# Low parts of weights on GpSimd from the pair loop to the end of the recurrence

## The chip, the cores and the metric

The kernel runs on one core of a Trainium2 chip, as one launch. The time is the device time of that launch in microseconds (us); less is better. TensorE (PE) does the matrix products; VectorE (DVE), ScalarE (ACT) and GpSimd (POOL) do the elementwise work; SyncE (SP) and ScalarE issue the transfers between the memory of the chip and SBUF. Each engine works off its own list of instructions in order, and waits in place when the next one is not ready.

## The reference

Two residual layers, each followed by a SwiGLU feed-forward block, over 1024 tokens of width 1024, all in float32. The first layer mixes by spatial gating and pooling and is not touched by the change. The second is RWKV-7 time mixing, and the change works there and in the feed-forward blocks that run beside it:

```python
def rwkv7_time_mix(h, ...):
    xx = shift(h) - h
    xr, xw, xk, xv, xa, xg = [h + xx * mu[i] for i in range(6)]
    r = xr @ w_r;  k = xk @ w_k;  v = xv @ w_v
    wlog = -softplus(-(w0 + tanh(xw @ w1) @ w2)) - 0.5
    a = sigmoid(a0 + (xa @ a1) @ a2)
    g = sigmoid(xg @ g1) @ g2
    kk = heads(k * k_k) / norm;  k = k * (1 + (a - 1) * k_a)
    # state: per head 64 x 64, one step per token
    #   sa = state @ (-kk);  state = state * w + sa (kk a)^T + v k^T;  y = state @ r
    y = wkv7_scan(r, exp(-exp(wlog)), k, v, -kk, kk * a)
    ...
    return (y * g) @ w_o

def swiglu(hn, w_gate, w_up, w_down):
    return (silu(hn @ w_gate) * (hn @ w_up)) @ w_down
```

## The kernel before

**Products in two parts.** TensorE runs in the fp32r format, which keeps fewer bits than float32. So each operand of a product is split into a high part (the fp32r rounding) and a low part (what the rounding left), and a product is three matmuls: high by high, high by low, low by high (`mm3`, lines 402 to 405). `split` (line 156) makes the two parts of a weight tile of 128x1024: ScalarE copies the loaded tile `raw` into the high part `whi` (line 157), and VectorE subtracts it from `raw` and writes the low part `wlo` (line 158). The tiles `raw`, `whi` and `wlo` have three buffers each. Weights are used in a fixed order, the list `plan`; `take` hands out the parts of one weight, and splits the next one and loads the one after it. Activations that were stored to memory and come back (`n0`, `n1`, `y`) go through the same list, with the low part named `alo`; weights of the down projection that go to buffers of their own have `wdhi` and `wdlo`.

**Halves and stages.** The 1024 tokens are worked on as two halves of 512. For each half the time mixing has these stages, and the feed-forward work of the other layer or the other half fills TensorE beside them:

1. The pair loop (`project`, lines 1305 to 1372). It runs over eight pairs of heads, p = 0 to 7. For each, TensorE multiplies by a block of `w_k` and one of `w_r` and by the low-rank weights; then a chain of short operations over ScalarE, GpSimd and VectorE makes decay, `ar` and `bk`: `sg` and `av` (GpSimd, line 1070), the running sum `cum` (VectorE, line 1331), exponentials (ScalarE), `ar` (VectorE, line 1354), `kkn` times `av` (GpSimd, line 1361) and from it `bk` (VectorE, line 1365). `interact` (line 1245, one pair later) is the TensorE product of `ar` and `bk` of one pair.
2. Two inversions of triangular 32x32 blocks (`invert`, line 1416), one for pairs 0 to 3, one for pairs 4 to 7. Each is a chain of 31 steps of two small VectorE operations, `it` (line 1427) and `xi` (line 1432), each waiting on the one before. It begins when `iat` has come back from memory (it needs `interact` of its last pair), and ends with a copy (line 1434) and the write of `xi` to memory (line 1436). There is one buffer `xi`: before the second inversion GpSimd clears it (memset, line 1421), which waits until the first one's write has left it.
3. The products with `w_v` (lines 1399 to 1401), eight weight tiles.
4. The recurrence (`recur`, line 1453) over eight chunks of 64 tokens, many small matmuls one after the other (lines 1475 and 1477), with feed-forward products in between. It starts with `load(0)`: transfers from the SP queue bring `ar`, `bk` and the rest of the first chunk; on that queue they stand behind the write of the second inversion's `xi`. The first matmul of the recurrence (`gram`, line 1477) needs `bk`.

**What sets the order.** The program is written in the order of `drive` and `beside`, which mix the steps of two generators; then a scheduler of the tile framework goes through it with a model of the times of each engine, and from that fixes the list of every engine before the launch. A change of engine for some instructions so also moves others that it does not name.

The element that selects the engine for a low part is the last argument of `split`:

Of the kernel before, what the change touches and what calls it, by code (L numbers as in the profile page):

```python
# [43 lines left out]
def tile_trunk(  # L44
# [8 lines left out]
    act, dve, pool, pe, sp = nc.scalar, nc.vector, nc.gpsimd, nc.tensor, nc.sync  # L53
# [53 lines left out]


    acts, dests, splits, makes = set(), {}, {}, {}

    def push(key, parts, view=lambda t: t, dest=None):
        plan.append((key, parts, view, dest))

    def load_at(i):
        if i >= len(plan) or i in raws:
            return
        if plan[i][0][0] in acts and plan[i][0][0] not in dests:
            return
        raw = wst.tile([P, D], F32, tag="raw", name="raw")
        for dst, src in plan[i][1]:  # L120
            act.dma_start(dst(raw), src)
        raws[i] = raw
# [4 lines left out]
    def split_at(i):  # L127
        if i >= len(plan) or i in ready:
            return
        load_at(i)  # L130
        if i not in raws:
            return
        key, _, view, dest = plan[i]
        if key[0] in makes:
            ready[i] = makes[key[0]](i)
            return
        raw = raws[i]
        to = (dest or whl)()
        if to is None:
            return  # L140
        hi, lo = to
        splits.get(key[0], lambda i, *t: split(*t))(key[1], view(raw), view(hi), view(lo))
        ready[i] = hi, lo

    def take(key):
        i = pos[0]
        assert plan[i][0] == key, (plan[i][0], key)
        pos[0] += 1
        split_at(i)
        load_at(i + 1)  # L150
        if i + 1 in raws:
            load_at(i + 2)
        split_at(i + 1)
        return ready.pop(i)

    def split(src, hi, lo, eng=None):
        act.activation(hi, src, AF.Copy)  # L157
        (eng or dve).tensor_tensor(out=lo, in0=src, in1=hi.bitcast(F32), op=ALU.subtract)  # L158
# [298 lines left out]
    def act_tiles(pool_, n=HT):  # L457
        return [pool_.tile([P, KT, n], F32R, tag=t, name=t) for t in ("ahi", "alo")]
# [231 lines left out]
    for h in range(2):  # L690
        hi, lo = act_tiles((xlp, actp)[h])
# [499 lines left out]
    def project(h, hn1, kp, ring, keep, before_v):  # L1191
# [3 lines left out]
        def tmp(tag, bufs=1, shape=None, dt=F32):  # L1195
            if early.get(tag):
                return early[tag].pop(0)
            return ep.tile(shape or [P, HT], dt, tag=tag, bufs=bufs, name=tag)
# [14 lines left out]
        for m in range(KT):  # L1213
# [4 lines left out]
            t = tmp(("k", "epx", "av", "sg")[m % 4], 2)  # L1218
# [3 lines left out]
        for n in range(2):  # L1222
            take(("wa2", n, h))

        twlo, talo = keep["twlo"], kp.tile([P, HT], F32R, tag="ghi", name="talo")
        act.activation(talo[rows[1]], twlo[rows[1]].bitcast(F32), AF.Copy)
        pool.memset(talo[rows[0]].bitcast(F32), 0.0)
# [160 lines left out]
        for cb in range(2):  # L1388
# [14 lines left out]
            for j in range(4):  # L1403
                t = tmp(("sg", "k", "kkn", "epx")[j], 2)
# [48 lines left out]
    def recur(h, wp, stream):  # L1453
# [271 lines left out]
        for c in range(8):  # L1725
# [3 lines left out]
                yield from post(c // 2)  # L1729
            yield BURST / 2  # L1730
        turned.pop()()
        yield 1.0

    early_o = {}
# [205 lines left out]
    nxt = {}  # L1940
    ps_es = open_psum("psp0", PROJ)
    project(0, hn1, kp, ring, keep, early("n0", "act1", xlp_es))
    for e in (ring_es, kp_es, np_es):
        e.close()
# [10 lines left out]
    prime_b, steps_b = down_steps(1, D0B[1], lambda f: whl(), hslot, True, spill_h, (next(between[0]) for _ in range(4)))  # L1955
    prime_b()
    drive(ffn(0, 1, nxt["hn"], f, D0P[:3], nd=2), recur(0, wp, in_pieces(hb_pool, 1, h_d[1, 0])), 6.2)
    wp_es.close()
    y, y_es = open_pool(name="y0", bufs=1, side="left")
# [36 lines left out]
    for e in (f_es, y_es, hb_es, ps_es):  # L1996
        e.close()
    ps_es = open_psum("psp1", PROJ)
    project(1, hn1, kp, ring, keep, early("n1", "act2", nxt["a_es"]))
    for e in (ring_es, kp_es, np_es):  # L2000
        e.close()
# [6 lines left out]
    f, f_es = open_pool(name="ffn2", bufs=1, side="right")  # L2008
    hnA = nxt["hn"]
    drive(ffn(1, 0, hnA, f, G1A[1], early=True), recur(1, wp, in_pieces(hp, 0, h_d[0, 1])), RATIO)  # L2010
    wp_es.close()
    ps_es.close()
# [48 lines left out]
```

## Time and profile before

| | |
|---|---|
| median of 3 runs | 2411.62 us (2407.74 to 2416.54) |
| the profiled execution, whole launch | 2410.52 us |
| its span from first to last instruction | 2408.8 us |
| TensorE busy in the span | 2327.8 us (97%) |
| VectorE, ScalarE, GpSimd busy | 1467.8, 947.7, 180.4 us |
| mean granted TensorE clock | 0.987 |

The span and the launch differ by 1.7 us, which lie before the first and behind the last instruction. The profile's page gives busy times and the costliest groups of instructions; a row of the timeline gives start, duration, engine, line, operation, and in brackets how long the engine had been idle and what it waited for; a row of the windows view gives, for a stretch of the span, the busy time of each engine with the number of instructions, the granted clock, the share of the transfer engines and GB/s. Lines are those of the kernel before; the kernel after has them one to three further down.

### The profile page before, as it was taken

The numbers are of one execution on the slowest core, as the hardware profiler recorded it, in microseconds if no ns is written. First come the engines' busy times: TensorE is split into PE (matmuls) and PEld (weight loads), VectorE is DVE, ScalarE is ACT, GpSimd is POOL, SyncE is SP. The second block draws the span as 40 slices with busy tenths as digits, with TensorE's granted clock in tenths as the row PEclk, the third lists the DMA queues.
The fourth block names the chain that finished last, engine by engine and source line by source line (L and its number), as shares of the span: only waits on it lengthen the run. The fifth ranks groups of instructions, "written<-read, shape, count | busy, mean of one in ns | idle before, by whom it ended". The sixth has DMA issues, their size and how long they took to land.

```text
span 2408.8 us, 37648 instructions
## 1 busy us (share of the span) xinstructions
PE 2327.8 (97%) x15315; PEld 1904.6 (79%) x15315; DVE 1467.8 (61%) x2312; ACT 947.7 (39%) x1427; POOL 180.4 (7%) x226
## 2 busy tenths in 40 slices
PE   8999999999999999989999899999899999999998
PEld 6888888888788787767867678777788787888887
DVE  6445775665568858847778758857654446434343
ACT  6233443444224755423337555423332224322223
POOL 0200000000000022001100022101100001000001
PEclk9999999999999999999999999999999999999999
DMA  5114452334765565774545565776434323433231
GB/s 180 53 46 146 149 163 84 126 101 150 276 227 192 162 180 134 224 206 146 157 131 143 173 159 146 212 223 169 133 110 134 109 81 96 138 98 99 80 106 52
DMA packets 408333, 342.73 MB, mean 142 GB/s; under 512 B 79392, under 2 KB 352928, under 8 KB 407392
## 3 DMA queue, kind: packets, MB, share of 16 engines
q10 hardware_dynamic: 266048, 195.33, 27.2%
q1 hardware_dynamic: 142112, 145.01, 19.3%
q8 instruction: 120, 1.97, 0.3%
q14 instruction: 53, 0.43, 0.1%
HBM read 263.33 MB, written 76.94 MB: 141 GB/s over the span
## 4 chain that ended last, share of the span: by engine, by line
PE 78%; DVE 8%; DMA 6%; issue 2%; ACT 2%; POOL 2%; SPq 1%; ACTq 0%; POOLq 0%; DVEq 0%
PE mm L403 17%; PE mm L404 17%; PE mm L405 17%; PE mm L734 5%; PE mm L736 5%; PE mm L735 5%; PE sm L1475 4%; DVE wlo L158 1%; DVE h L497 1%; PE yp L1475 1%; PE aux L1399 1%; PE mm L584 1%; PE mm L585 1%; PE aux L1400 1%; PE aux L1401 1%
## 5 line engine op out<-in xcount | busy, mean ns | idle before, releaser
L403 PE MATMUL mm<-ahi,whi 128*128 128x512 f32 x1376 | 543.2, 396 | 11.0 <-ACT whi L157 6.2
L404 PE MATMUL mm<-alo,whi 128*128 128x512 f32 x1376 | 542.9, 395 | 3.1 <-DVE alo L158 3.1
L405 PE MATMUL mm<-ahi,wlo 128*128 128x512 f32 x1376 | 541.6, 394 | 1.0 <-DVE wlo L158 0.9
L157 ACT ACTIVATE whi<-raw 128x1024 fp32r<-128x1024 f32 (+2 forms) x284 | 286.2, 1014 | 509.9 <-PE mm L404 385.8
L158 DVE TENSOR_TENSOR wlo<-raw,whi 128x1024 fp32r<-128x1024 f32 (+2 forms) x284 | 337.0, 1191 | 232.0 <-ACT whi L157 208.2
L403 PEld LDWEIGHTS mm<-ahi,whi 128*128 128x128 f32 x1376 | 259.8, 189 | 70.5 <-ACT whi L157 8.2
L404 PEld LDWEIGHTS mm<-alo,whi 128*128 128x128 f32 x1376 | 259.9, 189 | 60.3 <-DVE alo L158 4.5
L405 PEld LDWEIGHTS mm<-ahi,wlo 128*128 128x128 f32 x1376 | 259.9, 189 | 59.1 <-DVE wlo L158 3.1
L497 DVE TENSOR_TENSOR h<-h,mm 128x512 f32<-128x512 f32 x276 | 186.0, 684 | 158.5 <-PE mm L405 148.4
L403 PE MATMUL mm<-hidhi,wdhi 128*128 128x512 f32 x304 | 117.6, 394 | 4.8 <-ACT hidhi L962 3.0
L405 PE MATMUL mm<-hidhi,wdlo 128*128 128x512 f32 x304 | 119.3, 393 | 0.0
L404 PE MATMUL mm<-hidlo,wdhi 128*128 128x512 f32 x304 | 119.2, 393 | 0.1
L734 PE MATMUL mm<-ahi,whi 128*128 128x512 f32 x296 | 115.6, 390 | 0.0
L735 PE MATMUL mm<-alo,whi 128*128 128x512 f32 x296 | 115.2, 389 | 0.0
L736 PE MATMUL mm<-ahi,wlo 128*128 128x512 f32 x296 | 113.6, 389 | 0.0
L157 ACT ACTIVATE wdhi<-raw 128x1024 fp32r<-128x1024 f32 x42 | 43.3, 1057 | 162.2 <-PE mm L404 124.6
L959 DVE TENSOR_TENSOR sg<-sg,mm 128x512 f32<-128x512 f32 x52 | 35.7, 686 | 115.5 <-PE mm L405 115.4
L158 DVE TENSOR_TENSOR wdlo<-raw,wdhi 128x1024 fp32r<-128x1024 f32 x42 | 53.2, 1266 | 30.5 <-ACT wdhi L157 30.3
L403 PEld LDWEIGHTS mm<-hidhi,wdhi 128*128 128x128 f32 x304 | 57.1, 188 | 18.4 <-ACT hidhi L962 3.4
L405 PEld LDWEIGHTS mm<-hidhi,wdlo 128*128 128x128 f32 x304 | 57.4, 189 | 12.2 <-issue 0.3
L404 PEld LDWEIGHTS mm<-hidlo,wdhi 128*128 128x128 f32 x304 | 57.4, 189 | 12.2 <-DVE hidlo L963 0.5
L734 PEld LDWEIGHTS mm<-ahi,whi 128*128 128x128 f32 x296 | 55.6, 188 | 11.7 <-issue 0.2
(394 smaller groups left out, 4254.1 us busy)
## 6 DMA issues: line engine op xcount, KB each, us to landing
raw<-in_ffn_w_down_dram ACTq DMA_DIRECT2D x88, 512.0 KB
raw<-in_ffn_w_gate_dram ACTq DMA_DIRECT2D x74, 512.0 KB
raw<-in_ffn_w_up_dram ACTq DMA_DIRECT2D x74, 512.0 KB
hid_d<-hid SPq DMA_DIRECT2D x36, 512.0 KB
hd<-hid_d SPq DMA_DIRECT2D x26, 512.0 KB
raw<-in_ab_w_in_dram ACTq DMA_DIRECT2D x16, 512.0 KB
raw<-in_ab_w_out_dram ACTq DMA_DIRECT2D x16, 512.0 KB
raw<-in_rwkv_w_r_dram ACTq DMA_DIRECT2D x16, 512.0 KB
```

The source lines that it names most:

```text
L157: act.activation(hi, src, AF.Copy)
L158: (eng or dve).tensor_tensor(out=lo, in0=src, in1=hi.bitcast(F32), op=ALU.subtract)
L403: pe.matmul(o, whi, xhi, start=first, stop=False)
L404: pe.matmul(o, whi, xlo, start=False, stop=False)
L405: pe.matmul(o, wlo, xhi, start=False, stop=last)
L497: dve.tensor_tensor(out=H[h][:, m, :], in0=H[h][:, m, :], in1=o, op=ALU.add)
L584: pe.matmul(ops[j], xhi[:, k, sl], whi[:, kk], start=(k == 0), stop=False)
L734: pe.matmul(o, wh[:, k, :], x[0][:, k, :], start=st, stop=False, skip_group_check=True)
L735: pe.matmul(o, wh[:, k, :], x[1][:, k, :], start=False, stop=False, skip_group_check=True)
L736: pe.matmul(o, wl[:, k, :], x[0][:, k, :], start=False, stop=k == 3, skip_group_check=True)
L959: dve.tensor_tensor(out=s, in0=s, in1=o, op=ALU.mult)
L1475: i = f(*args, **kw)
```

## The change

A cell `low_on` names the engine that makes the low part when a weight of the list is split. It starts as VectorE. When `project` has taken its low-rank weights, just ahead of the pair loop, it is set to GpSimd; when the recurrence has recorded its last step, it is set back to VectorE. This happens once for each half. Low parts that are made without the list (`mix_steps`, `split_steps`, `norm_split`, hidden activations) stay on VectorE. The choice falls on everything of the list that is split in that stretch, so the returning activations `n0` and `n1` go to GpSimd too.

```diff
     acts, dests, splits, makes = set(), {}, {}, {}
+    low_on = [dve]
...
         hi, lo = to
-        splits.get(key[0], lambda i, *t: split(*t))(key[1], view(raw), view(hi), view(lo))
+        splits.get(key[0], lambda i, *t: split(*t, low_on[0]))(key[1], view(raw), view(hi), view(lo))
         ready[i] = hi, lo
...
         for n in range(2):
             take(("wa2", n, h))
 
+        low_on[0] = pool
         twlo, talo = keep["twlo"], kp.tile([P, HT], F32R, tag="ghi", name="talo")
...
                 yield from post(c // 2)
             yield BURST / 2
         turned.pop()()
+        low_on[0] = dve
         yield 1.0
```

109 subtractions of 128x1024 change engine: 89 `wlo`, 12 `wdlo` and 8 `alo`. The lists change at more places than these.

On GpSimd, at the end of the pair loop of the first half, pair 7, the list was

```order
L1070 TENSOR_SCALAR av<-av 128x512
L1337 COPY pct<-epx 128x8
L1358 TENSOR_SCALAR ar<-kkn 128x8
L1361 TENSOR_TENSOR kkn<-kkn,av 128x512
L1421 MEMSET xi 128x2048
L1469 MEMSET S 128x512
```

and is now

```order
L1339 COPY pct<-epx 128x8
L159 TENSOR_TENSOR wlo<-raw,whi 128x1024
L159 TENSOR_TENSOR alo<-raw,ahi 128x1024
L1360 TENSOR_SCALAR ar<-kkn 128x8
L1423 MEMSET xi 128x2048
L1363 TENSOR_TENSOR kkn<-kkn,av 128x512
L159 TENSOR_TENSOR alo<-raw,ahi 128x1024
L159 TENSOR_TENSOR wlo<-raw,whi 128x1024 x3
```

Beside the subtractions that came in, the memset of `xi` moved from behind the product `kkn` of pair 7 to ahead of it. The second half's list changed in the same way.

On TensorE, at the first matmul of the recurrence in the first half (`sm` is its PSUM tile), the list was

```order
L403 MATMUL mm<-hidhi,whi 128x512
L404 MATMUL mm<-hidlo,whi 128x512
L405 MATMUL mm<-hidhi,wlo 128x512
L1477 MATMUL sm<-ar,bk 64x128
L1475 MATMUL sm<-ar,bk 64x128 x31
```

and is now

```order
L404 MATMUL mm<-ahi,whi 128x512
L405 MATMUL mm<-alo,whi 128x512
L406 MATMUL mm<-ahi,wlo 128x512
L1479 MATMUL sm<-ar,bk 64x128
L1477 MATMUL sm<-ar,bk 64x128 x31
```

The matmul stood within a group of the down projection (`hid`) and now stands within the gate and up products ahead of it (`a`). Between `interact` of pair 7 and this matmul there were 288 matmuls of 128x512 in the first half and 308 in the second; there are now 225 and 230.

On VectorE, at the end of the first inversion of the first half, the last `bk` of the pair loop stood in the middle of the inversion's steps:

```order
L1354 SCALAR_TENSOR_TENSOR ar<-kkn,epx 128x8x63
L1432 TENSOR_TENSOR xi<-xi,it 128x7x25
L158 TENSOR_TENSOR alo<-raw,ahi 128x1024
L1171 TENSOR_TENSOR xlo<-mix,xhi 128x512
L1178 SCALAR_TENSOR_TENSOR mix<-hn_5522,vec,mix 128x512
L1427 TENSOR_TENSOR it<-iat,xi 128x156
L1365 TENSOR_TENSOR bk<-kkn,em 128x8x64
```

It now stands behind the inversion's closing copy:

```order
L1434 TENSOR_TENSOR xi<-xi,it 128x31
L1436 COPY xi<-xi 128x32x32
L1172 TENSOR_TENSOR xlo<-mix,xhi 128x512
L1371 TENSOR_TENSOR ar<-mm,epx 128x8x64
...
L1356 SCALAR_TENSOR_TENSOR ar<-kkn,epx 128x8x63
...
L1367 TENSOR_TENSOR bk<-kkn,em 128x8x64
```

So eleven of the inversion's small operations and its copy moved from behind this `bk` to ahead of it (rows left out are further `xlo` and `mix`).

## The prediction

> **What bounds the kernel now.** I read the busy times by stretch: the pair loop and the recurrence of each half, which the change touches, and for comparison a dense stretch.
>
> ```profile
> 842.00:992.00 150.00, 146.22 (x910) 121.15 (x909) 108.33 (x175) 81.59 (x123) 37.38 (x46) 0.99 0.66 182
> 992.00:1240.00 248.00, 234.52 (x3313) 190.66 (x3312) 171.67 (x371) 82.18 (x139) 24.77 (x23) 0.98 0.53 151
> 1382.00:1535.00 153.00, 146.75 (x899) 121.19 (x899) 105.50 (x172) 80.86 (x122) 36.47 (x43) 0.97 0.62 167
> 1535.00:1800.00 265.00, 249.91 (x3369) 204.01 (x3368) 174.01 (x367) 88.66 (x147) 24.22 (x24) 0.99 0.56 160
> 300.00:400.00 100.00, 100.00 (x443) 82.84 (x442) 67.54 (x98) 42.59 (x66) 0.00 (x0) 1.00 0.39 127
> ```
>
> The columns after the length are PE, PEld, DVE, ACT, POOL. TensorE bounds every stretch. In the four that the change touches it idles 3.8, 13.5, 6.2 and 15.1 us, 38.6 together; more than that no faster VectorE can give back. The dense row gives the price of a 128x512 matmul: 100 us / 443 = 0.226 us. Who made TensorE wait, over the whole span:
>
> ```profile
> PE sm L1475 <- DVE gt L1522: 12.6, 5, 6.7
> PE aux L1245 <- DVE bk L1365: 6.6, 5, 2.0
> PE sm L1477 <- DMA bk<-bk_d: 5.5, 2, 3.3
> ...
> PE sm L1475 <- DVE XT L1563: 2.4, 1, 2.4
> ```
>
> VectorE causes 15.0 us of it in the recurrence (`gt`, `XT`). The third row is the first matmul of each recurrence, which waits for its load; it decides below. The engine that gets the work, GpSimd, has room: 37 of 150 us busy in the pair loop. What counts is the order that it must keep, and what its reads do to VectorE.
>
> **The price of one low part.**
>
> ```profile
> L158 DVE TENSOR_TENSOR wlo<-raw,whi 128x1024 fp32r<-128x1024 f32 x254 | 316.6, 1248 | 230.8 <-ACT whi L157 207.6 <-PE aux L1320 10.6 <-PE mm L405 5.2
> L1361 POOL TENSOR_TENSOR kkn<-kkn,av 128x512 f32<-128x512 f32 x16 | 21.7, 1359 | 4.2 <-DVE ar L1354 3.1
> L1660 POOL TENSOR_TENSOR vch<-vch,bon 128x1024 f32<-128x1024 f32 x8 | 15.3, 1915 | 108.9 <-DMA vch<-v_d 96.7 <-DMA XT<-xi_d 12.2
> L668 POOL TENSOR_TENSOR zw<-zw 128x525 f32<-128x525 f32 x6 | 6.4, 1062 | 28.2 <-DVE zw L668 10.9 <-DVE zq L675 9.0 <-DVE zp L658 8.3
> ```
>
> On VectorE it is 1.25 us (1.22 undisturbed). The trace has none on GpSimd. From below it is bounded by the same size with a small second operand (1.92), from above by two of the 128x512 products (2.7); two additions of 128x525 give 2.1. A subtraction is nearest to the addition and to the full size row, so I take 2.0. [...]
>
> **The two engines hold each other up.** The rows of both, in the pair loop:
>
> ```profile
> 892.90 1.29 POOL L1361 TENSOR_TENSOR kkn<-kkn,av 128x512 f32<-128x512 f32 x1
> 893.23 2.04 DVE L158 TENSOR_TENSOR wlo<-raw,whi 128x1024 fp32r<-128x1024 f32 x1
> ...
> 916.59 0.63 POOL L1070 TENSOR_SCALAR sg<-sg 128x512 f32<-128x512 f32 x1 [5.58 <-ACT sg L1324]
> 916.61 0.70 DVE L1432 TENSOR_TENSOR xi<-xi,it 128x87 f32<-128x87 f32 x1
> 972.86 0.25 DVE L1432 TENSOR_TENSOR xi<-xi,it 128x87 f32<-128x87 f32 x1
> 959.30 4.17 POOL L1358 TENSOR_SCALAR ar<-kkn 128x8 f32<-128x8 f32 x1 [3.20 <-ACT kkn L1353]
> ```
>
> A low part on VectorE that began during a GpSimd product took 2.04 instead of 1.22. A step of the inversion took 0.70 behind a GpSimd operation and 0.25 alone; the steps wait on one another, which leaves gaps, and GpSimd got in at once with its usual 0.63. So in an inversion a GpSimd operation stops VectorE for nearly its length. A low part there would cost the chain 2.0 less about 0.25 (the step already under way) = 1.75, against 1.15 that it takes now (1.22 less an overlap with its neighbours). The engine is relieved of the instruction and pays more for it. The last row is the other case: VectorE ran filled without gaps, and GpSimd took 4.17 for what takes 0.74. [...]
>
> **Term 1: `kkn` of pair 7 behind the memset of `xi`.**
>
> ```profile
> 905.30:976.20 70.90, 12.98 (x10) 0.98 0.57 146
> 988.30:1024.30 36.00, 9.82 (x9) 1.00 0.60 186
> 1533.90:1575.60 41.70, 14.64 (x12) 1.00 0.69 209
> ...
> 963.55 1.83 POOL L1361 TENSOR_TENSOR kkn<-kkn,av 128x512 f32<-128x512 f32 x1
> 966.15 1.97 PE L1245 MATMUL aux<-ar,bk 64*64 64x64 f32 x32 [2.01 <-DVE bk L1365]
> 975.11 1.06 DVE L1434 COPY xi<-xi 128x1024 f32<-128x1024 f32 x1
> 986.75 1.82 POOL L1421 MEMSET xi<- 128x2048 f32 x1 [21.38 <-DMA xi_d<-xi]
> ...
> 1513.45 1.15 PE L1245 MATMUL aux<-ar,bk 64*64 64x64 f32 x32 [2.01 <-DVE bk L1365]
> 1522.41 1.10 DVE L1434 COPY xi<-xi 128x1024 f32<-128x1024 f32 x1
> 1530.76 1.82 POOL L1421 MEMSET xi<- 128x2048 f32 x1 [18.08 <-DMA xi_d<-xi]
> ```
>
> The first three rows are VectorE's low parts alone, in the stretches of the first inversion of the first half and of the second inversion of each half: 10, 9 and 12. `interact` of pair 7 already waits 2.0 us for `bk`, which needs `kkn`. Now `kkn` stands behind the memset, and this behind the write of the first inversion, which freed it 10.6 us after the copy in the first half (986.75 - 976.17) and 7.2 in the second. When will the copy end? It ended at 976.2; ten low parts leave VectorE, 13.0 us, and about 5 us of pair 7's work now stands behind it: 958 if GpSimd costs VectorE nothing. If all ten hold it for 1.75, it is 975.7. I take the middle, 967, plus 7.2 for the write, 1.8 for the memset, 1.3 for `kkn`, and 0.7 to the start of `interact`: 978 against 966.15, **+12 us**. The ends are +3.5 (958 and 7.2) and +24 (975.7 and 10.6). Behind `kkn` on GpSimd wait the low parts of the last `w_v` tiles, needed later than `interact`. The second half has the same list and gets the same +12.
>
> **Term 2: the recurrence starts too early in TensorE's list.**
>
> ```profile
> 988.37 0.70 DVE L1268 TENSOR_SCALAR iat<-iat 128x32 f32<-128x32 f32 x1 [2.91 <-DMA iat<-n_d]
> 1023.23 1.08 DVE L1434 COPY xi<-xi 128x1024 f32<-128x1024 f32 x1
> 1037.40 0.29 PE L1477 MATMUL sm<-ar,bk 64*64 64x128 f32 x1 [2.16 <-DMA bk<-bk_d]
> ...
> 1533.94 0.18 DVE L1268 TENSOR_SCALAR iat<-iat 128x32 f32<-128x32 f32 x1 [3.03 <-DMA iat<-n_d]
> 1574.45 1.11 DVE L1434 COPY xi<-xi 128x1024 f32<-128x1024 f32 x1
> 1588.92 0.29 PE L1477 MATMUL sm<-ar,bk 64*64 64x128 f32 x1 [3.33 <-DMA bk<-bk_d]
> ```
>
> From `interact` of pair 7 the load's way is: 22.2 us to the start of the second inversion (966.15 to 988.37), 35.9 for it, 13.1 for the write, the load of `ar` and that of `bk`, which follow one another on SP's queue: 71.2. TensorE needs 69.1 to get there and so waits 2.2. In the new list it has 63 matmuls fewer ahead, 14.2 us: it arrives after 54.9. The inversion loses nine low parts (9 times 1.15 less rounding, 9.1 us: 26.8), and GpSimd's are made meanwhile: TensorE's work left over in that time, 54.9 - 22.2 = 32.7, uses six weight tiles of 24 matmuls (5.4 us), and two `alo` come with them; eight times 1.75 is 14.0: 40.8. The load lands after 22.2 + 40.8 + 13.1 = 76.1, a wait of 21.2, **+19.0 us**. With GpSimd for nothing it is 62.1, a wait of 7.2 and +5.0; with 2.0 a piece +21.
>
> Second half: 20.5 to the inversion, 41.6, 13.4; TensorE's 72.1 shrink by 78 matmuls (17.6) to 54.5. The inversion: 41.6 - 13.7 + 14.0 = 41.9. The wait is 75.8 - 54.5 = 21.3, less the 3.3 of now: **+18.0**, between +4.0 and +20.
>
> **Term 3: relief.** In the recurrence `gt` and most of VectorE's work reads PSUM, and about thirty low parts a half leave it. Of the 15.0 us that TensorE waits for VectorE there I take 12 as won, between 0 and 15. The longest (6.7) is one wait. The other low parts of the pair loop and the recurrence lie beside TensorE's work, made two tiles ahead; uncovered, each would cost up to 2.0.
>
> **Sum.** 12 + 19 + 12 + 18 - 12 = +49 on the profiled launch of 2410.5, which lies 1.1 below the median: **2459.5 us**. Its own range from the ends of the terms is 2411 to 2500.
>
> **Rivals.**
> 1. *The scheduler's order holds* (on the other side). It decides if GpSimd's low parts don't stop the inversions. With the low ends, 3.5 + 5 + 3.5 + 4 - 15 = +1; and if write and loads land as early as the new lists suppose, the waits at `bk` (4.0) and at the loads (5.5) go as well: -24.5. Middle 2399. For it: in the first half the transfer engines were 60% busy during the second inversion, and the lists before met the chip within 2 to 3 us. Against it: the rows 0.70 and 2.04.
> 2. *GpSimd stands in line in the recurrence.* Its low parts stand behind products `vch` that waited 97 us in all for their transfers, and behind the memsets of `XT`. If each of the eight `vch` holds the next weight up by 3.5 us beyond its lead, 28 us come on top: 2487. Against it: TensorE's place in its list frees these waits.
> 3. *GpSimd starves*, as in the 4.17 row: then the inversions are short (low ends, 16 us), but low parts come late; half of 3.4 us for eight in each half is 27: 2410.5 + 16 + 27 - 12 = 2441.
>
> **Chances.** Forecast 0.45, rival 1 0.27, rival 2 0.16, rival 3 0.12. A difference under 0.3% (7.2 us) can't be told from none. Faster holds most of rival 1, 0.19; within, 0.11; slower, 0.70. The range over the cases is 2403 to 2490: it leaves out the better half of rival 1 and the end of rival 2.
>
> **What would show it.** Right: TensorE's waits for `bk` at `interact` of pair 7 of some 14 us, released by GpSimd's `kkn` behind the memset; waits for the load of `bk` of about 20 us at the first matmul of each recurrence; steps `it` and `xi` stretched to about 2 us beside GpSimd's low parts of 1.9 to 2.3; VectorE's busy time down by about 130 us less what the stops add. Wrong: second inversions under 30 us, or a launch under 2411.

## The result, and the profile after

The change makes the kernel slower: 2490.14 us (median of 4 runs, 2484.62 to 2492.22) against 2411.76 us, a ratio of 1.0318 with a 95% interval of 1.0297 to 1.0339. The forecast was 2459.5; the time lies at the upper edge of the range, 2403 to 2490. The direction was right, and 78 us were lost where 48 were forecast.

The profiled execution of the changed kernel has a span of 2487.3 us, 78.5 more than before. Its page begins with the busy times:

```profile
PE 2348.4 (94%) x15315; PEld 1918.8 (77%) x15315; DVE 1481.2 (60%) x2203; ACT 948.0 (38%) x1427; POOL 440.2 (18%) x335
```

VectorE has 109 instructions fewer and is busy for 13.4 us *more* than before. TensorE does the same 15315 matmuls in 20.6 us more (2348.4 against 2327.8), at a granted clock of 0.972 instead of 0.987, and idles 57.9 us more.

To see where the time went I cut each half into three stretches that begin and end at the same instructions: A from the first `interact` to that of pair 7, B from there to the first matmul of the recurrence, C from there to the end of the recurrence (its last matmul, `sm` from `ysb`). The windows view of the kernel before:

```profile
861.00:966.10 105.10, 101.37 (x681) 83.60 (x681) 80.66 (x133) 55.83 (x87) 28.44 (x33) 1.00 0.58 150
966.10:1037.40 71.30, 69.09 (x329) 57.19 (x329) 52.29 (x106) 27.48 (x36) 3.51 (x6) 0.98 0.76 227
1037.40:1234.90 197.50, 186.96 (x3105) 151.88 (x3106) 131.20 (x282) 65.61 (x118) 23.93 (x20) 0.97 0.51 145
1403.00:1513.40 110.40, 105.44 (x680) 87.02 (x680) 82.72 (x136) 56.18 (x87) 28.78 (x34) 0.95 0.57 147
1513.40:1588.90 75.50, 72.14 (x348) 59.64 (x349) 55.58 (x110) 30.38 (x39) 3.05 (x5) 1.00 0.79 228
1588.90:1796.00 207.10, 195.32 (x3128) 159.12 (x3129) 129.56 (x274) 67.48 (x122) 23.00 (x20) 0.98 0.52 146
```

and of the changed kernel:

```profile
863.30:983.90 120.60, 105.56 (x672) 86.61 (x671) 92.46 (x135) 57.62 (x90) 61.22 (x49) 0.93 0.55 141
983.90:1055.50 71.60, 56.38 (x265) 46.19 (x266) 52.20 (x73) 20.39 (x25) 34.12 (x18) 0.88 0.64 188
1055.50:1268.00 212.50, 193.06 (x3121) 157.05 (x3121) 130.37 (x263) 67.73 (x122) 56.35 (x34) 0.95 0.49 141
1444.30:1568.80 124.50, 105.77 (x674) 87.26 (x673) 94.32 (x136) 57.80 (x90) 63.35 (x49) 0.92 0.54 138
1568.80:1643.60 74.80, 56.93 (x271) 46.74 (x271) 53.62 (x73) 21.83 (x26) 36.66 (x18) 0.89 0.59 170
1643.60:1859.00 215.40, 203.03 (x3134) 164.74 (x3135) 119.77 (x251) 70.57 (x126) 75.49 (x42) 0.96 0.51 146
```

The lists differ, so a stretch doesn't hold the same number of matmuls. I charge the difference at 0.226 us a matmul: stretch B of the first half lasts as long as before, but does 64 matmuls fewer, which are 14.5 us of work put off. The forecast's relief of 12 is split evenly over the two halves.

| | A | B | C | sum |
|---|---|---|---|---|
| first half, forecast | +12 | +19 | -6 | +25 |
| first half, measured | 15.5 + 2.0 = +17.5 | 0.3 + 14.5 = +14.8 | 15.0 - 3.6 = +11.4 | +43.7 |
| second half, forecast | +12 | +18 | -6 | +24 |
| second half, measured | 14.1 + 1.4 = +15.5 | -0.7 + 17.4 = +16.7 | 8.3 - 1.4 = +6.9 | +39.1 |

Together 82.8, against a loss of 78.5; the rest lies outside, above all between the two halves, where the changed kernel wins 4.0 by the same count. A and B come out at 64.5 where 61 were forecast. The 30 us that the forecast lacks lie in C, the recurrence: the relief of 12 didn't come, and 18 were lost there instead.

TensorE's waits in the changed kernel, over the whole span:

```profile
PE sm L1479 <- DMA bk<-bk_d: 31.4, 2, 17.2
PE aux L1247 <- DVE bk L1367: 27.2, 6, 7.2
PE sm L1477 <- ACT uv L1599: 8.2, 2, 8.0
PE sm L1477 <- DVE gt L1524: 8.1, 3, 4.0
...
PE sm L1477 <- DVE Q L1577: 4.9, 3, 3.1
...
PE sm L1477 <- DVE XT L1565: 4.0, 5, 1.7
PE sm L1477 <- DVE w L1551: 4.0, 1, 4.0
```

The first is the first matmul of each recurrence (5.5 before), the second is `interact` (6.6 before), the third was 1.2 before. `gt` has fallen from 12.6, but the three other waits for VectorE in the recurrence have grown: `Q` from 0.2, `XT` from 2.4, and `w` wasn't among them. The four together are 21.0 us, where they were 15.2.

**Who holds whom in A and B.** GpSimd's and VectorE's rows, in the first and then in the second inversion of the first half:

```profile
940.27 2.44 POOL L159 TENSOR_TENSOR wlo<-raw,whi 128x1024 fp32r<-128x1024 f32 x1 [1.87 <-ACT whi L158]
940.43 2.83 DVE L1367 TENSOR_TENSOR bk<-kkn,em 128x512 f32<-128x512 f32 x1
943.32 1.97 PE L1247 MATMUL aux<-ar,bk 64*64 64x64 f32 x32 [7.00 <-DVE bk L1367]
...
1020.58 2.56 POOL L159 TENSOR_TENSOR wlo<-raw,whi 128x1024 fp32r<-128x1024 f32 x1 [1.70 <-ACT whi L158]
1020.47 0.41 DVE L1434 TENSOR_TENSOR xi<-xi,it 128x240 f32<-128x240 f32 x1
1020.91 2.50 DVE L1429 TENSOR_TENSOR it<-iat,xi 128x247 f32<-128x247 f32 x1
```

A step of 0.41 becomes 2.50 beside a low part of 2.56, and `bk`, 0.68 before, becomes 2.83: what VectorE starts during these two subtractions of GpSimd ends only 0.3 and 0.6 us after they have ended. TensorE, at `interact` of pair 5, has waited 7.0 us by then. GpSimd's low parts in the two second inversions (rows of that line alone), and the ends of these inversions:

```profile
995.10:1045.10 50.00, 0.00 (x0) 27.86 (x11) 0.99 0.56 169
1573.60:1632.90 59.30, 0.00 (x0) 35.43 (x14) 0.99 0.56 165
...
995.17 0.18 DVE L1270 TENSOR_SCALAR iat<-iat 128x32 f32<-128x32 f32 x1 [0.83 <-DMA iat<-n_d]
1044.09 1.01 DVE L1436 COPY xi<-xi 128x1024 f32<-128x1024 f32 x1
```

Eleven and fourteen low parts stand in them (28 and 35 us of GpSimd), and they last 49.9 us (995.17 to 1045.10; 36.0 before) and 59.2 us (41.6 before), although VectorE makes no low part of a weight there any more. Within these lengths VectorE also idles until the rest of `iat` has come, 0.9 us in the first half and 6.6 in the second; before the change it didn't.

**Who holds whom in C.** One place in the first half's recurrence, followed over three engines:

```profile
1109.85 2.38 POOL L159 TENSOR_TENSOR wlo<-raw,whi 128x1024 fp32r<-128x1024 f32 x1
1124.22 1.90 POOL L1662 TENSOR_TENSOR vch<-vch,bon 128x1024 f32<-128x1024 f32 x1 [12.00 <-DMA vch<-v_d]
1126.08 2.34 POOL L159 TENSOR_TENSOR wlo<-raw,whi 128x1024 fp32r<-128x1024 f32 x1
...
1128.45 0.39 ACTq L122 DMA_DIRECT2D raw<-in_ffn_w_up_dram  x1
1128.94 0.59 ACT L1599 ACTIVATE uv<-sm 64x512 f32<-64x512 f32 x1 [8.72 <-POOL wlo L159]
...
1129.58 0.48 PE L1477 MATMUL sm<-uv,bkt 128*64 128x64 f32 x2 [7.95 <-ACT uv L1599]
```

GpSimd's product `vch` waits 12.0 us for its transfer. The low part behind it starts when it is done, and frees its tile `raw` at 1128.4. ScalarE issues the loads of weights, and its next load command (the ACTq row) wants that tile; behind the command stands the copy `uv`, and for `uv` TensorE waits 7.95 us. So a low part that is late on GpSimd stops TensorE through ScalarE's list, though no matmul waits for that low part. That the load command waits for this tile is read from the times: it starts 0.03 us after the low part has ended.

### The profile page after: what moved, and what is told of

Same layout as the page of the kernel before. It is cut to its first block, busy times and chain, and to the rows that moved or that the text cites. A ratio compares the mean times of both kernels' runs of the same rounds, so it can differ in the third digit from the quotient of the medians.

```text
span 2487.3 us, 37691 instructions
## 1 busy us (share of the span) xinstructions
PE 2348.4 (94%) x15315; PEld 1918.8 (77%) x15315; DVE 1481.2 (60%) x2203; ACT 948.0 (38%) x1427; POOL 440.2 (18%) x335
## 3 DMA queue, kind: packets, MB, share of 16 engines
q10 hardware_dynamic: 266048, 195.33, 26.5%
q8 instruction: 120, 1.97, 0.3%
## 4 chain that ended last, share of the span: by engine, by line
PE 72%; DVE 14%; DMA 6%; ACT 3%; issue 2%; POOL 2%; SPq 1%; ACTq 1%; POOLq 0%; DVEq 0%
PE mm L404 16%; PE mm L405 16%; PE mm L406 16%; PE mm L735 5%; PE mm L737 5%; PE mm L736 5%; PE sm L1477 4%; DVE it L1429 3%; DVE xi L1434 3%; DMA raw<-y_d 1%; DVE xlo L1172 1%; DVE mix L1179 1%; PE yp L1477 1%; POOL wlo L159 1%; ACT whi L158 1%
## 5 line engine op out<-in xcount | busy, mean ns | idle before, releaser
L159 DVE TENSOR_TENSOR wlo<-raw,whi 128x1024 fp32r<-128x1024 f32 (+2 forms) x195 | 222.5, 1146 | 166.5 <-ACT whi L158 158.0
L404 PEld LDWEIGHTS mm<-ahi,whi 128*128 128x128 f32 x1376 | 261.4, 190 | 69.4 <-ACT whi L158 5.3
L159 POOL TENSOR_TENSOR wlo<-raw,whi 128x1024 fp32r<-128x1024 f32 x89 | 218.7, 2459 | 241.5 <-ACT whi L158 230.0
L409 POOL TENSOR_TENSOR nrs<-nrs,small 128x4 f32<-128x4 f32 x8 | 8.5, 1067 | 508.2 <-DVE nrs L445 508.2
L1789 POOL TENSOR_TENSOR u<-turn,fgb 128x512 f32<-128x512 f32 x8 | 11.5, 1433 | 377.7 <-ACT fsq L1786 357.4
L1429 DVE TENSOR_TENSOR it<-iat,xi 128x31 f32<-128x31 f32 (+15 forms) x124 | 76.0, 613 | 3.5
L1434 DVE TENSOR_TENSOR xi<-xi,it 128x31 f32<-128x31 f32 (+15 forms) x124 | 72.0, 580 | 3.4
```

Source lines behind the costliest of these rows:

```text
L404: pe.matmul(o, whi, xhi, start=first, stop=False)
L1429: dve.tensor_tensor(out=t, in0=bc(iat[:, j, j + 1 : 32].unsqueeze(2), sh), in1=bc(xi[:, j, 0 : j + 1].unsqueeze(1), sh), op=ALU.mult,)
L1434: dve.tensor_tensor(out=xs, in0=xs, in1=t, op=ALU.add)
```

## The experiments

Three theories were set against one another. **Port**: while GpSimd reads the two tiles of a low part, VectorE is kept out. **Order**: the new lists are what costs, the recurrence's early place in TensorE's list above all. **Line**: in the recurrence a low part stands in GpSimd's list behind work that waits, and holds ScalarE's list. The last was formed after the first four runs. All runs are compared with the kernel before, run on the same chip (2409 to 2413 us).

### Only the pair loop, only the recurrence

```diff
 # the pair loop only (on the change), in recur
+        low_on[0] = dve
         load(0)
 # the recurrence only (on the change), in project and in recur
-        low_on[0] = pool
         twlo, talo = keep["twlo"], kp.tile([P, HT], F32R, tag="ghi", name="talo")
...
+        low_on[0] = pool
         load(0)
```

> GpSimd makes the low parts only from the pair loop to the end of w_v; the recurrence has them on VectorE again. Set against each other at equal work done by TensorE, the two traces so far lose about 20 and 18 us in the pair loops, 23 and 23 at the first recurrence matmuls, and win back 4 and 1 in the recurrences. Theory 'port' (GpSimd's low parts keep VectorE out, in the inversions above all): nearly all of the loss stays, 2411.7 + 84 less what the recurrences lose themselves, 2485 to 2497. Rival 'recurrence' (the weights that GpSimd makes beside the recurrence are what comes late): most of the loss is gone, under 2450.

> GpSimd makes the low parts only in the recurrence. In TensorE's list the first recurrence matmul stands 273 and 272 big matmuls behind the last interact, against 288 and 308 before and 225 and 230 in the change. Theory 'port': the relief of 5 us (4 and 1) stays, 2403 to 2410, and both second inversions are as long as before, 36 and 42 us. The prediction's Term 3 by itself: 12 us faster, 2400. Rival 'recurrence': over 2440.

Measured: 2451.05 (ratio 1.0160, 1.0138 to 1.0183) and 2458.48 (1.0202, 1.0178 to 1.0225). Both expectations of "port" missed, from the two sides: the pair loop alone costs 41 us, not nearly all, and the recurrence alone costs 49, where I had expected a gain (the rival had put it over 2440). So the recurrence has a cost of its own, which the traces of before and after hide. In the second run the second inversions take 38.7 and 42.5 us, about as before, and TensorE waits for `uv` for 18.2 us in three stretches; in the two long ones, 9.1 and 6.7 us, GpSimd shows the chain above again, with `vch` waiting 11.5 and 10.6 us for its transfer. That led to "line". The profiled execution of this run took 2467.7 us, 9 more than the median, so its trace shows somewhat more than the run lost. The two parts add up to 90, more than the 78 of both. By the count of the stretches the excess lies in B and C of the second half: 11.6 and 31.6 us for the parts, 23.6 for both. Why isn't known.

### No low part of GpSimd in an inversion

```diff
                 inv.append(invert(h, p - 3, iat, tmp))
+                low_on[0] = dve
...
                 if next(inv[0], "end") == "end":
                     inv.pop(0)
+            low_on[0] = dve if inv else pool
```

> As the change, but while an inversion is under way the low parts are VectorE's. Gram 0 stands 265 and 268 big matmuls behind the last interact. Theory 'port': inversions of about the length they had before, interact of pair 5 no longer 7 us late; what stays is a few us in pairs 0 to 3 and 20 to 40 matmuls less to cover the load: 2415 to 2430. Rival 'queue' (the pair's own products sg, av and kkn stand behind low parts in GpSimd's order, and that is what costs, in every pair): 2440 or more, with waits for bk as in the change.

Measured: 2440.30 (1.0127, 1.0106 to 1.0147). Stretch A of both halves, in the columns of the stretches above:

```profile
862.40:966.20 103.80, 99.48 (x674) 82.06 (x673) 78.73 (x130) 55.36 (x86) 37.87 (x37) 1.00 0.58 150
1416.70:1524.90 108.20, 102.47 (x672) 84.48 (x671) 80.22 (x131) 55.92 (x86) 38.91 (x37) 0.97 0.57 145
```

103.8 and 108.2 with 7 and 8 matmuls fewer: the loss in A is gone (+0.3 and -0.4), though GpSimd still makes the low parts of the first pairs, and `cum` still waits for GpSimd's `sg` for 52.0 us in all (49.7 in the change). That is "port" against the queue of the pair's own products; against "order" this run says less, since its list has the memset of `xi` behind `kkn` again, as before. The time as a whole, though, lies where the rival had put it, 10 us above the range of "port". The order of the program isn't that of the run: six and eight low parts of the recurrence's first weights still ran on GpSimd in the two second inversions, which took 41.1 and 45.2 us. By the count of the stretches B lost 9.1 and 10.7 us and C 7.2 and 6.7, the latter with only 1.3 us of waits for `uv` in the whole run.

### The recurrence's first matmul later in TensorE's list

```diff
+        dmm[0] = pe.matmul(o, wlo, xhi, start=False, stop=last)   # in mm3
-        yield 0.2
+        yield 0.2 + (5, 5)[h] * (6.2, RATIO)[h]
+        last.append(dmm[0].ins)
         gram(0, 0)
```

> As the change, but the first recurrence matmul is tied behind a later matmul of the dense block: it stands 287 and 279 big matmuls behind the last interact, instead of 225 and 230. Theory 'order': the waits of 14.2 and 17.2 us for bk are filled by 62 and 49 matmuls (14.0 and 11.1 us), and TensorE isn't slowed to half its clock afterwards (some 6 us each): 2490 - 25 - 10 = 2455, between 2450 and 2468. Rival 'length' (what the inversion takes longer is only put off to the next load or to gt): 2480 or more, the wait turning up later in the recurrence.

Measured: 2530.72 (1.0488, 1.0460 to 1.0515), 41 us slower than the change. "Order" fell in the form that was set down. The waits at the load vanished, and others took their place:

```profile
PE mm L404 <- ACT sg L952: 14.6, 2, 7.5
PE mm L404 <- ACT hidhi L963: 10.8, 2, 8.3
```

The feed-forward products that were to fill the wait need VectorE themselves: in the first half the product `sg` that `hidhi` is made from stood in VectorE's list behind the inversion, and ScalarE's `hidhi` waited 9.2 us for it. So putting this one matmul back wins nothing: part of what then stands ahead of it waits for the inversion too.

### The reading alone

```diff
 # the reading alone, in split
-        (eng or dve).tensor_tensor(out=lo, in0=src, in1=hi.bitcast(F32), op=ALU.subtract)
+        dve.tensor_tensor(out=lo, in0=src, in1=hi.bitcast(F32), op=ALU.subtract)
+        if eng is pool:
+            for c in range(4):
+                cs = slice(c * 256, c * 256 + 256)
+                pool.tensor_tensor(out=spare, in0=hi[:, cs].bitcast(F32), in1=hi[:, cs].bitcast(F32), op=ALU.subtract)
 # the writing alone, ahead of the subtraction in split
+        if eng is pool:
+            for _ in range(2):
+                pool.memset(lo.bitcast(F32), 0.0)
+            return
```

> VectorE makes all low parts, as before; GpSimd, where the change has it make one, reads the high part as both operands in four pieces of 128x256 and writes a spare tile that nobody reads. So nobody waits for GpSimd's result, no raw tile is freed later, and VectorE is relieved of nothing; only GpSimd's reading and its place in GpSimd's own order stay. Gram 0 at 285 and 308, as before. Theory 'port': the second inversions, 36 and 42 us, grow by 2 us for each of 8 to 12 such readings to 55 to 65, interact is late in the pair loop, 2460 to 2510. Rival 'order' (the loss comes from the new lists and from what waits for GpSimd's low parts): under 2430.

> As the change, but GpSimd writes zeros into the low part, twice (it leaves out these 109 low parts): about 1.8 us of GpSimd for each instead of 2.4, and nothing read. Gram 0 stands at 212 and 220. Theory 'port' (what stops VectorE is the reading of two tiles): the second inversions, 50 and 59 us in the change, fall to 28 to 34, interact of pair 5 isn't late, and of the loss of 79 us the 35 to 40 of the recurrence's line stay: 2435 to 2455. Theory 'queue' (GpSimd's time alone counts): inversions of 45 us or more and 2470 to 2490.

Measured: 2474.27 (1.0252, 1.0229 to 1.0274) with the reading, and 2422.49 (1.0051, 1.0034 to 1.0069) with writing alone. The 31 steps `it` of the second inversion of the first half, grouped: the kernel before, the change, the reading, and the writing.

```profile
L1427 DVE TENSOR_TENSOR it<-iat,xi 128x31 f32<-128x31 f32 (+15 forms) x31 | 10.6, 342 | 0.9
...
L1429 DVE TENSOR_TENSOR it<-iat,xi 128x31 f32<-128x31 f32 (+15 forms) x31 | 23.1, 744 | 1.1
...
L1434 DVE TENSOR_TENSOR it<-iat,xi 128x31 f32<-128x31 f32 (+15 forms) x31 | 16.9, 545 | 0.8
...
L1433 DVE TENSOR_TENSOR it<-iat,xi 128x31 f32<-128x31 f32 (+15 forms) x31 | 10.6, 342 | 1.1
```

342 ns a step alone, 744 beside GpSimd's low parts, 545 beside its readings (of 0.86 us a piece), and 342 again beside memsets that take GpSimd 1.97 us for each tile. Stretches A and B with the reading:

```profile
862.50:980.70 118.20, 104.08 (x671) 84.72 (x670) 98.00 (x138) 57.75 (x91) 73.92 (x89) 0.95 0.54 138
980.70:1066.50 85.80, 72.34 (x329) 58.63 (x330) 67.87 (x105) 24.87 (x31) 54.65 (x69) 0.94 0.60 181
1445.80:1564.80 119.00, 105.70 (x673) 86.11 (x672) 97.75 (x138) 57.80 (x91) 73.83 (x89) 0.94 0.54 137
1564.80:1656.30 91.50, 79.08 (x352) 63.80 (x352) 75.34 (x109) 28.02 (x34) 69.48 (x83) 0.91 0.60 182
```

By the same count A loses 15.4 and 10.2 and B 14.5 and 15.1, 55 us together against 64.5 in the change. Here VectorE makes all low parts, TensorE's list has the recurrence where it was, and no matmul uses what GpSimd writes. The second inversions take 50.3 and 59.5 us, where the kernel before, which also has VectorE's low parts in them, takes 36.0 and 41.6. So the reading is enough for most of the loss in A and B. Two limits: GpSimd's readings take 3.45 us for a low part instead of 2.46, and somebody did wait for them (ScalarE, 52.9 us in all, for high parts that GpSimd was still reading), against the expectation. In the recurrence this kernel loses little: TensorE waits for `uv` 2.6 us in the first half.

The writing alone came out below its own range. It reads nothing and so holds no `raw` tile, which takes away "line" with "port"; its stretch A of the first half lasts 106.1 us with four matmuls more than before, no loss. It is still 13 us slower than the kernel before, though VectorE is relieved of 109 operations: neither "port" nor "line" explains these 13 us, and the new lists may be what costs them.

### The waiting work out of GpSimd's list

The first try moved that work to VectorE, with the same move in the kernel before as the control, and with the third run's rule as the hoped-for best version:

```diff
 # on the recurrence alone, on the kernel before, and on the one without low parts in an inversion
-            pool.tensor_tensor(out=v16, in0=v16, in1=bc(b16...), op=ALU.mult)
+            dve.tensor_tensor(out=v16, in0=v16, in1=bc(b16...), op=ALU.mult)
-                pool.memset(XT[b0 + 32 : b0 + 64, :, 0:32], 0.0)
+                dve.memset(XT[b0 + 32 : b0 + 64, :, 0:32], 0.0)
```

> As the run with GpSimd's low parts in the recurrence alone (2458.5, +48.5 on before), but the product vch and the memsets of XT, which wait for transfers and for TensorE ahead of them in GpSimd's order, are VectorE's. Gram 0 keeps its place in TensorE's list, 273 and 272. Theory 'line' (a low part stands behind vch or XT, frees its raw tile late, ScalarE's next load command waits for that tile, and uv and ysb stand behind the command): the waits of ScalarE for GpSimd's wlo, wdlo and XT, 42 us in all there, mostly go, and the time falls to 2415 to 2430. Rival 'port' (the recurrence is slow because low parts keep VectorE out): no change, 2450 to 2465.

> The kernel before with the same two moves alone (vch and XT's memsets on VectorE, all low parts on VectorE): the control. VectorE gets 8 products of about 1.25 us and 32 small memsets and is not the bound: 2408 to 2420 by either theory.

> Low parts on GpSimd from the pair loop to the end of the recurrence except while an inversion is under way (2440.3 measured), with vch and XT's memsets on VectorE. Both causes removed: by 'port' in the inversions and 'line' in the recurrence 2405 to 2420, which could be under before. If the recurrence loses for another reason, 2435 or more.

Measured: 2472.38 (1.0260), 2448.39 (1.0166, 1.0144 to 1.0187) and 2477.57 (1.0283). The control, expected at 2420 at most, says why the other two tell nothing: the move itself costs 39 us. `vch` now waits on VectorE:

```profile
DVE vch L1660 <- DMA vch<-v_d: 34.7, 8, 5.8
```

34.7 us in which nothing behind it on VectorE runs. Here, as on GpSimd, the product that waits for its transfer holds the list that it stands in.

The second try gave `vch` two buffers, so that its load could start earlier; once on the recurrence alone, once with no low part in an inversion:

```diff
 # on the recurrence alone, and on the one without low parts in an inversion
-            vch = wt("vch", 1, [P, 2, 8, 64])
+            vch = wt("vch", 2, [P, 2, 8, 64])
```

> Low parts on GpSimd in the recurrence alone (2458.5, +48.5), with two buffers for vch instead of one, so that its load doesn't wait for the last vch to be used, and GpSimd's product and the low part behind it don't wait for the load. VectorE and TensorE's list are left as they are (gram 0 at 273 and 272). Theory 'line' (low part behind vch, ScalarE's load command behind the low part's raw tile, uv behind the command): the two stretches of 9 us in which TensorE waits for uv go, with the clock behind them, and the time falls to 2425 to 2442; the waits behind XT's memsets stay. Rival 'port' (low parts keep VectorE out of the recurrence): 2450 to 2465.

> Low parts on GpSimd from the pair loop on except while an inversion is under way (2440.3), with two buffers for vch. With 'line' and 'port' both right: the pair loop loses nothing as in that run, the recurrence loses less: 2412 to 2428. If the recurrence loses by the port: 2436 or more.

Measured: 2451.06 (1.0154, 1.0133 to 1.0175) and 2442.78 (1.0109, 1.0087 to 1.0132). The first is 7 us better than with one buffer, the second isn't better at all; both came out in the range of "port" and not of "line". But the wait that was to go had gone only in part: ahead of its eight products GpSimd still idled 52.8 us (64.1 with one buffer) in the first and 37.3 (64.0) in the second. What held the loads then stays open. TensorE's waits for `uv` stayed with the wait: 18.8 us against 18.2 in the first. In the second there was no line to take away, since TensorE waited for `uv` for only 1.3 us there even with one buffer. So these two runs neither show the line nor refute it; what the second still loses has another cause.

The third try leaves the product out, and writes XT's zeros once:

```diff
 # on the recurrence alone
-            pool.tensor_tensor(out=v16, in0=v16, in1=bc(b16...), op=ALU.mult)
-            xx = wt("XT", 2, [P, 8, 96])
+            xx = XS.setdefault(c % 2, None) or wt("XT", 2, [P, 8, 96])
+            XS[c % 2] = xx
+                if c < 2:
                     pool.memset(XT[b0 + 32 : b0 + 64, :, 0:32], 0.0)
```

> Low parts on GpSimd in the recurrence alone (2458.5, +48.5), and everything taken out of GpSimd's order that waited there for a transfer or for TensorE: the product vch is left out (the output lacks the bonus term), and XT's zeros are written once in each of its two buffers instead of for each chunk. VectorE's work is as in that run, gram 0 at 273 and 272. Theory 'line': ScalarE's waits for wlo and wdlo under 10 us in all (some 40 before), no wait of TensorE for uv over 3 us, 2415 to 2435; what stays is the second half's gram 0 (about 10 to 20 us). Rival 'port' (VectorE kept out for 2.4 us at a time is what lengthens the recurrence): 2445 to 2460.

Measured: 2431.22 (1.0069, 1.0046 to 1.0092), 27 us of the 49 gone, inside the range of "line". Stretch C of both halves with the waiting work in GpSimd's list:

```profile
1043.30:1260.80 217.50, 196.92 (x3126) 159.28 (x3127) 132.28 (x273) 66.43 (x120) 51.98 (x32) 0.95 0.46 133
1620.30:1846.00 225.70, 206.21 (x3127) 168.56 (x3128) 119.39 (x251) 69.43 (x124) 74.21 (x41) 0.93 0.47 135
```

and without it:

```profile
1045.70:1247.60 201.90, 192.87 (x3127) 155.75 (x3128) 133.06 (x273) 66.34 (x120) 40.76 (x16) 0.98 0.49 143
1597.60:1813.80 216.20, 203.69 (x3137) 166.24 (x3138) 119.55 (x252) 69.35 (x124) 63.07 (x25) 0.96 0.50 142
```

15.6 us less in the first half and 9.5 in the second, with VectorE's work and GpSimd's low parts the same. TensorE's waits for `uv` fell from 18.2 us (longest 9.1) to 5.1 (longest 2.6). ScalarE's waits for GpSimd's low parts didn't fall under 10 as I had written; about 36 us are left, none longer than 4.6, and what went are two long ones behind `vch`, 10.4 and 8.5 us, which the view puts down to the memset of `XT` right behind the low part. One thing isn't parted from the line: the product itself reads two tiles on GpSimd for 1.9 us, eight times, and the kernel before wasn't run without it. So the line is shown for the waits for `uv`, 13 us in the profiled executions; the rest, slower matmuls among it, may in part be what the product costs by itself. What is still lost lies mostly in B, probably by the low parts of the recurrence's first weights.

No version beat the kernel before. The nearest that computes everything is the one without low parts in the inversions, 30 us slower.

## Why the prediction was right and wrong

**The mutual hold: right, and the core of it.** It was read from two rows (0.70 for 0.25, 2.04 for 1.22); the runs with reading and with writing alone show it: a step `it` of the second inversion took 545 ns in the mean beside the readings, and 342 beside the memsets as in the kernel before. The two large groups of products with one operand in PSUM weren't held (690 ns at most), below.

**The price of a low part on GpSimd: undersized.** 2.0 forecast, 2.46 measured (89 `wlo`, mean 2459 ns).

**Term 1, +12 each half: right in size (17.5 and 15.5), wrong in its mechanism.** That the size fits is luck. The step that failed is "`kkn` of pair 7 behind the memset of `xi`":

```profile
978.95 0.67 POOL L1360 TENSOR_SCALAR ar<-kkn 128x8 f32<-128x8 f32 x1
979.70 1.81 POOL L1423 MEMSET xi<- 128x2048 f32 x1
981.47 1.27 POOL L1363 TENSOR_TENSOR kkn<-kkn,av 128x512 f32<-128x512 f32 x1
```

The memset waited for nothing and cost 1.8 us; the write that frees `xi` had landed before. Pair 7 was late by then: of its 17.8 us, 13.5 were there at pair 5 already (943.32 against 929.86; 2.3 of them from ahead of A), whose `bk` was held in the first inversion. TensorE waited 7.0 us for `bk` at pair 5 in both halves, and 3.5 and 7.2 at pair 7, where 14 were forecast. The run with the reading alone had the memset behind `kkn` again, and lost 15.4 in the first half. I had costed the hold for the inversion's steps only, and not for the pair's own products that VectorE makes between them. (The low end of this term was added up as 3.5; its parts make 2.9.)

**Term 2, +19 and +18: right within 4 us (14.8 and 16.7), with two terms off that cancel, which is luck.** The way of the load was forecast as 22.2 + 40.8 + 13.1 = 76.1. It was 11.2 + 49.9 + 10.4 = 71.5 in the first half and 4.9 + 59.2 + 10.8 = 74.9 in the second. `interact` of pair 7, being late, comes closer to the second inversion than before: the first inversion had ended by then, where before it ended 10 us behind `interact`. And the inversion is longer: 11 and 14 low parts instead of 8, since low parts of the recurrence's weights run there too. Each cost about 2.0 and 1.9 us, not far from the 1.75 forecast: (49.9 - 0.9 - 26.5) / 11 and (59.2 - 6.6 - 26.5) / 14, without the wait for the rest of `iat`, and with 26.5 us for such an inversion in the run with the writing alone. So it was above all their number that the forecast had wrong, and less the hold. The first half's sum has a slip as well: nine low parts at 1.15 are 10.4 and not 9.1, which would have made the term +17.7. TensorE waited 14.2 and 17.2 us for the load, where 21 were forecast, and each wait had a slow stretch behind it (2.7 and 5.1 us at a granted clock of 0.50). The early place in the list, which I named as the cause, isn't shown to cost anything: putting the place back won nothing, and the run with the reading alone, with the place as before, lost 14.5 and 15.1 us in B all the same.

**Term 3, -12: this is where the forecast failed.** I took 12 of the 15.0 us that TensorE waits for VectorE in the recurrence as won. `gt` did fall, from 12.6 to 8.1 us, but with `Q`, `XT` and `w` these waits came to 21.0 us where they had been 15.2: there was no relief, though about thirty low parts a half had left VectorE, and C lost 11.4 and 6.9 us. I had also put GpSimd's line behind `vch` aside as a rival with a chance of 0.16, arguing that TensorE's place in its list frees it. Its price was near the 30 us that were missing (28), but that is chance: I looked for it in the low part being late for TensorE, and where the line shows, it works through the tile `raw` and ScalarE's load command. The runs show it with the recurrence alone; in the changed kernel itself I can show the one place above, 8.0 us in the first half. In its second half TensorE idles in C about as long as before (12.4 against 11.8), and nearly all of the 6.9 us are slower matmuls. The run without low parts in the inversions lost about as much in that stretch, 6.7 us, and 7.2 in the first half, with hardly a wait for `uv`. So what the line explains of C in the changed kernel is that one wait; the cause of the rest stays open.

**The clock: not in the forecast.** 20.6 of the 78.5 us are the same matmuls done slower. In the 14.2 us of waiting before the first half's recurrence the granted clock was 1.00 for 3.3 us and 0.50 for the rest, 0.62 in the mean, and it stayed at 0.50 for 2.7 us behind the wait; the first matmuls there took 0.44 us where the same ones took 0.29 before. In the 17.2 us of the second half it was 1.00 for 5.3 us and then 0.50, and it stayed so for 5.1 us behind the wait. (The expectation of the run with this matmul put back has some 6 us for each.) I had given such stretches behind stalls no term. In the kernel before, where TensorE waited 2.2 and 3.3 us at these places, the first half had such a stretch too, 3.4 us at 0.50 that began 0.4 us behind the wait, and the second had none. What makes the clock fall these runs don't show.

**The rivals.** The first (the scheduler's order holds) would have needed GpSimd to stop nothing; the run with writes alone comes nearest to that, and at 2422 even it isn't faster than before. The third (GpSimd starves) isn't seen: the 89 `wlo` took 2.40 us in the median and 3.76 at most, a delay of 1.4 us where this rival reckoned with 3.4.

## What to carry to other kernels

An engine that is busy for only 7% of the time, as GpSimd was here, isn't free: ask what its reads stop on the other engine, above all where that engine works through a chain of short steps, and ask what each moved instruction stands behind in its new list. Follow a late instruction by everything that it frees, not only by its result: here TensorE once waited 8 us for a source tile, through the load command of a third engine. And look for a second price of a new long stall of TensorE in the matmuls behind it: here the granted clock was 0.50 for 2.7 and 5.1 us behind the waits of 14.2 and 17.2 us, and slower matmuls, over the whole span, were a quarter of the loss (20.6 of 78.5 us).

## What the runs showed of the hardware

The two large groups of VectorE's products that read one operand from PSUM were not held by GpSimd's low parts. In the changed kernel the longest of the 52 products `sg` took 690 ns and the longest of the 276 sums `h` as much, and before the change they took 689 and 690; the five `h` and the one `sg` that began within a low part took 686 to 689. Of VectorE's products with both operands in SBUF `bk` went from a mean of 682 to 1140 ns and `k` from 680 to 1384. So a relief could be had beside instructions of the first kind at most, and the inversion, with both operands in SBUF, is a bad place for it. A copy with its one operand in SBUF was held as well: `xi` from `iat`, 128x32, took 2.28 us beside a low part in the second inversion of the first half, and 0.20 in the other three; before the change it took 0.17 to 0.19.

Clearing a tile on GpSimd (1.97 us for two memsets of 128x1024) left VectorE's steps at 342 ns. And shorter pieces cost a step less than long ones: beside four readings of 0.86 us for each tile a step took 545 ns in the mean, beside whole low parts 744, though GpSimd read for 32.2 us in that inversion against 27.9 in the change. The inversion as a whole was no shorter (50.3 us against 49.9); there VectorE made its low parts as well.
